# Loading each ranked expert's number into a SyncE register next to the first weight load that uses it

## The chip, the cores and the metric

The kernel runs on one core of one Trainium2 chip. The metric is the device time of one execution in microseconds (us); less is better. A number given for a kernel is the median of its runs. The profile is of one further execution, which has its own time.

## What is computed

The reference is a two-layer trunk over 256 latent tokens and 256 context tokens of width 1024, all in 32-bit floats. Layer 0 is attention and a dense SwiGLU; layer 1 is a short gated convolution and then a mixture of experts, which is the part that matters here:

```python
logits = h @ router_w                                  # 256 tokens x 8 experts
top_vals, top_idx = lax.top_k(logits, 2)
weights = softmax(top_vals)
gates = sum(one_hot(top_idx, 8) * weights[..., None])
for e in range(8):                                     # each expert: 1024 -> 3584 -> 1024
    out += gates[:, e] * ((silu(h @ w_gate[e]) * (h @ w_up[e])) @ w_down[e])
```

Each token uses two of the eight experts. All eight experts' weights, 352 MB of the 470 MB that the kernel reads, pass through the core once.

## The kernel before

**Experts by rank.** The experts are worked in the order of ranks 0 to 7. Rank 0 is always expert 0, so its weights can be read before the router's answer is there. Ranks 1 to 7 are the other experts, sorted by how many tokens chose them; ranks 0 to 4 are "heavy" (a tile of 128 tokens, weights split in two parts for exactness), ranks 5 to 7 "light" (64 tokens). Each expert is cut into 7 chunks. A list `chunks` fixes the order of the 56 chunks: four heavy chunks of rank 0, then heavy and light mixed, at last four light ones. So which rank comes when is known as the program is built; which expert a rank stands for is known only on the chip. The DVE computes it in `ranks` (L1165) into the tile `idx`, and SyncE (SP) needs it in registers to form the address of a weight load.

**Weight loads.** Every weight tile is a DMA of 1 MB, issued by SP with `load` (L61) into a buffer `raw` out of a ring of pools, in the fixed order of the list `order`: for each chunk two `moe_g` and two `moe_u` tiles, with two `moe_d` tiles of the chunk before. In `feed` (L110) an entry of `order` that is a function is called to give the source; `weights` (L91) makes these functions, which look the expert's register up in `who`. At one place the tiles named `xhat` and `late` and four buffers of further pools join the ring (L117), so that more loads can be in flight. A load waits for the last reader of its buffer's old content, and for the load eight places earlier to land. SP runs its instructions strictly in the order of the program.

**Conversion and matmuls.** A loaded tile of a heavy chunk is taken in two halves of 128x1024: ScalarE (ACT) writes a rounded part `hi` (L71), VectorE (DVE) the rest `lo` (L72), into five buffers, and TensorE (PE) multiplies `hi` and `lo` in groups of three matmuls at L267, L269 and L271. `ahead(4)` (L133) converts up to four halves before the one in use. Light chunks go straight to PE (L1316).

**The first chunk.** Chunk 0 has eight parts p = 0 to 7 on PE, one for each half tile: two for the first `moe_g` tile, two for the first `moe_u`, two for the second `moe_g`, two for the second `moe_u`. The first three of these tiles are loaded before the router's work is done. The hook at (0, 1) (L1412) runs `ranks` in part 1; with it, in the program's order, stand the seven loads of `idx` into registers. The hook at (0, 3) turns positions into rank order (`by_rank`, L1193), the one at (1, 1) computes the gates (`gates`, L1199), both small DVE work. The schedule is written by hand: each engine's order is the order of the code.

Of the kernel before, what the change touches and what calls it, by code (L numbers as in the profile page):

```python
# [19 lines left out]
NE = 8  # L20
# [13 lines left out]
def trunk(ctx, tc, i, out, dbg=None):  # L34
    nc = tc.nc
# [11 lines left out]
    cur = {}  # L47
# [4 lines left out]
    def pm():  # L52
        return cur["pm"].tile([128, 512], F32, name="pm")
# [35 lines left out]
    who, whole = {}, []  # L89

    def weights(m, r, c, h):  # L91
        return lambda: i[m][who[r] if r else 0, c, h]

    whole += [False] * len(order)
    for n in range(len(chunks) + 1):
        if n < len(chunks):
            order += [weights(m, *chunks[n], h) for h in range(2) for m in ("moe_g", "moe_u")]
            whole += [chunks[n][0] >= NE - NL] * 4
        if n:
            order += [weights("moe_d", *chunks[n - 1], h) for h in range(2)]  # L100
            whole += [chunks[n - 1][0] >= NE - NL] * 2
# [1063 lines left out]
    def ranks():  # L1165

        n = pm()
        pe.matmul(n[:, 0:8], ones, sl[:, 0], start=True, stop=False)
        pe.matmul(n[:, 0:8], ones, sl[:, 1], start=False, stop=True)
        key, rank, ids, long = (m1.tile([128, NE], F32, name=v) for v in ("key", "rnk", "ids", "long"))  # L1170
        cmp = m1.tile([128, NE, NE], F32, name="cmp")
        idx = m1.tile([128, NE], I32, name="idx")
        most = m1.tile([128, 1], F32, name="most")
        io = iota[:, 0:NE]
        dve.scalar_tensor_tensor(key, n[:, 0:8], 16.0, io, op0=OP.mult, op1=OP.subtract)
        dve.memset(key[:, 0:1], 1e6)
        dve.tensor_tensor(cmp, key[:, None, :].to_broadcast([128, NE, NE]), key[:, :, None].to_broadcast([128, NE, NE]),
                          op=OP.is_ge)
        dve.reduce_sum(rank, cmp, axis=AX.X)
        dve.tensor_tensor(perm, rank[:, None, :].to_broadcast([128, NE, NE]), io[:, :, None].to_broadcast([128, NE, NE]),  # L1180
                          op=OP.is_equal)
        dve.tensor_mul(cmp, perm, io[:, None, :].to_broadcast([128, NE, NE]))
        dve.reduce_sum(ids, cmp, axis=AX.X)
        dve.tensor_scalar(idx, ids, 1.0, None, op0=OP.subtract)
        for r in range(1, NE):
            who[r] = nc.values_load(idx[0:1, r:r + 1], engines=[mybir.EngineType.SP], min_val=0, max_val=NE - 1)
        dve.tensor_scalar(cap, rank, NE - NL + 0.5, CAP - 128.0, op0=OP.is_gt, op1=OP.mult)
        dve.tensor_scalar(cap, cap, 128.0, None, op0=OP.add)
        dve.tensor_tensor(long, n[:, 0:8], cap, op=OP.is_gt)
        dve.reduce_max(most, long, axis=AX.X)  # L1190
        dve.tensor_scalar(over, most, 0.5, None, op0=OP.is_gt)
# [205 lines left out]
    def down(C, s):  # L1397
# [10 lines left out]
        else:  # L1408
            k = slice(s * 128, (s + 1) * 128)
            mac(E.accs, C.dh[:, k], C.dl[:, k], *halves(ahead(4)), first, end)  # L1410

    hook(0, 1, ranks)  # L1412
    hook(0, 3, by_rank, posr, pos)
    hook(1, 1, gates)
# [4 lines left out]
    for n, (r, c) in enumerate(chunks):  # L1419
# [8 lines left out]
        for p in range(8):  # L1428
# [11 lines left out]
            half, m, j = p // 4, (p // 2) % 2, p % 2  # L1440
# [27 lines left out]
    for t in range(NT):  # L1468
        for q in range(2):
            c = slice(512 * q, 512 * q + 512)  # L1470
# [158 lines left out]
```

## Time and profile before

| what | us |
|---|---|
| median of 3 runs (1416.14, 1416.44, 1419.62) | 1416.44 |
| the profiled execution, its own time | 1419.48 |
| the profiled execution, span on the core | 1417.7 |
| PE busy (97% of the span) | 1380.8 |
| DVE busy (70%) | 990.7 |
| ACT busy (56%) | 791.0 |
| SP's one wait for the expert numbers, line 1186 | 51.4 |

The page gives the busy time of each engine over the span and, in 40 slices of 35.4 us, how busy each engine and the DMA were and how many GB/s they moved. PE is nearly always busy, and the chain of work that ended last is PE for 92% of the span. Where PE is idle is seen only in a narrower window; where a wait of SP shows, the question is whether PE needed what SP was about to load.

### The profile page before, as it was taken

What the parts mean: (1) busy time and instruction counts of PE and PEld (TensorE: products, weight loads), DVE (VectorE), ACT (ScalarE), POOL (GpSimd) and SP (SyncE); (2) the same over time, 40 slices, a digit from 0 to 9 for tenths busy, and PEclk for the clock granted to TensorE, in tenths of its full rate; (3) what the DMA queues carried; (4) which work ended last, traced back from release to release, by engine and by line L of the source; (5) the groups of instructions that cost most, each with busy time, mean ns of one, the idle gap of its engine ahead of it and who ended that gap; (6) DMA issues with size and microseconds to landing.
All of it is one profiled execution on the core that took longest, in us unless ns stands there. A gap on an engine that the chain in (4) does not pass through costs nothing.

```text
span 1417.7 us, 20577 instructions
## 1 busy us (share of the span) xinstructions
PE 1380.8 (97%) x7764; PEld 1020.5 (72%) x7764; DVE 990.7 (70%) x1341; ACT 791.0 (56%) x1070; POOL 0.2 (0%) x4
## 2 busy tenths in 40 slices
PE   6999999999999979999999999999999999999997
PEld 4776789999899968866666766767667676676742
DVE  4777769788777659866767767767577677676731
ACT  5567674444464348756556656656567566465610
POOL 0000000000000000000000000000000000000000
PEclk9999999999999989999999999999999999999999
DMA  9734778678756049999899999989989999998994
GB/s 368 275 120 132 255 297 298 237 300 306 254 222 254 31 166 421 421 421 421 367 423 421 420 406 368 401 340 386 420 335 413 420 415 371 359 420 368 411 421 171
DMA packets 66060, 469.81 MB, mean 331 GB/s; under 512 B 7328, under 2 KB 7968, under 8 KB 10016
## 3 DMA queue, kind: packets, MB, share of 16 engines
q1 hardware_dynamic: 65952, 468.41, 82.7%
q8 instruction: 63, 1.03, 0.3%
q14 instruction: 45, 0.37, 0.1%
HBM read 467.33 MB, written 1.05 MB: 330 GB/s over the span
## 4 chain that ended last, share of the span: by engine, by line
PE 92%; ACT 3%; DVE 3%; DMA 1%; issue 1%; SPq 0%; DVEq 0%; ACTq 0%
PE pm L1316 11%; PE pm L267 9%; PE pm L269 9%; PE pm L271 9%; PE acc L267 8%; PE acc L269 8%; PE acc L271 8%; PE acc L1316 5%; PE pm L923 4%; PE pm L925 4%; PE pm L924 4%; PE pm L1296 2%; PE pm L1258 2%; PE pm L177 1%; PE pm L1336 1%; PE pt L687 1%
## 5 line engine op out<-in xcount | busy, mean ns | idle before, releaser
L72 DVE TENSOR_TENSOR lo<-raw,hi 128x1024 fp32r<-128x1024 f32 x522 | 627.2, 1222 | 133.3 <-ACT hi L71 109.5
L71 ACT ACTIVATE hi<-raw 128x1024 fp32r<-128x1024 f32 x522 | 545.6, 1060 | 257.6 <-PE pm L271 113.0
L267 PE MATMUL pm<-hi,eh 128*128 128x512 f32 x560 | 225.6, 403 | 6.9 <-ACT hi L71 6.7
L269 PE MATMUL pm<-lo,eh 128*128 128x512 f32 x560 | 219.6, 392 | 2.1 <-DVE lo L72 2.1
L271 PE MATMUL pm<-hi,el 128*128 128x512 f32 x560 | 219.1, 391 | 0.0
L1316 PE MATMUL pm<-raw,hl 128*64 128x512 f32 x672 | 155.6, 599 | 0.0
L923 PE MATMUL pm<-th,hi 128*128 128x256 f32 x480 | 135.1, 281 | 0.0
L924 PE MATMUL pm<-tl,hi 128*128 128x256 f32 x480 | 134.6, 280 | 0.0
L925 PE MATMUL pm<-th,lo 128*128 128x256 f32 x480 | 134.6, 280 | 0.0
L267 PEld LDWEIGHTS pm<-hi,eh 128*128 128x128 f32 x560 | 105.5, 188 | 40.0 <-issue 8.8
L269 PEld LDWEIGHTS pm<-lo,eh 128*128 128x128 f32 x560 | 105.7, 189 | 24.7 <-DVE lo L72 4.6
L271 PEld LDWEIGHTS pm<-hi,el 128*128 128x128 f32 x560 | 105.5, 188 | 22.7
L1316 PEld LDWEIGHTS pm<-raw,hl 128*64 128x64 f32 x672 | 44.1, 136 | 79.8 <-issue 76.9
L923 PEld LDWEIGHTS pm<-th,hi 128*128 128x128 f32 x480 | 90.8, 189 | 1.2 <-issue 0.8
L924 PEld LDWEIGHTS pm<-tl,hi 128*128 128x128 f32 x480 | 90.7, 189 | 0.4
L925 PEld LDWEIGHTS pm<-th,lo 128*128 128x128 f32 x480 | 90.8, 189 | 0.0
L267 PE MATMUL acc<-hi,dh 128*128 128x512 f32 x280 | 88.6, 398 | 0.0
L269 PE MATMUL acc<-lo,dh 128*128 128x512 f32 x280 | 86.5, 390 | 0.0
L271 PE MATMUL acc<-hi,dl 128*128 128x512 f32 x280 | 86.3, 389 | 0.0
L1310 DVE TENSOR_TENSOR sg<-pm,sg 128x512 f32<-128x512 f32 (+1 forms) x56 | 38.6, 688 | 63.2 <-ACT sg L1309 62.9
L1316 PE MATMUL acc<-raw,dT 128*64 128x512 f32 x336 | 78.1, 600 | 0.0
L1309 ACT ACTIVATE sg<-pm 128x512 f32<-128x512 f32 (+1 forms) x56 | 32.8, 585 | 69.5 <-PE pm L1316 66.4
(323 smaller groups left out, 1646.4 us busy)
## 6 DMA issues: line engine op xcount, KB each, us to landing
raw<-in_moe_d_dram SPq DMA_DIRECT2D x112, 1024.0 KB, 11.2
raw<-in_moe_g_dram SPq DMA_DIRECT2D x111, 1024.0 KB, 11.5
raw<-in_moe_u_dram SPq DMA_DIRECT2D x111, 1024.0 KB, 11.0
raw<-in_ada_w_dram SPq DMA_DIRECT2D x48, 1024.0 KB, 6.3
raw<-in_conv_i_dram SPq DMA_DIRECT2D x12, 1024.0 KB, 6.9
raw<-in_ffn_g_dram SPq DMA_DIRECT2D x11, 1024.0 KB, 6.3
raw<-in_ffn_u_dram SPq DMA_DIRECT2D x11, 1024.0 KB, 5.1
raw<-in_ffn_d_dram SPq DMA_DIRECT2D x11, 1024.0 KB, 4.9
```

Of the source, the lines that this page charges most:

```text
L71: act.activation(hi, r, AF.Copy)
L72: dve.tensor_sub(lo, r, hi.bitcast(F32))
L267: pe.matmul(p, hh, wh[j], start=first, stop=False)
L269: pe.matmul(p, hh, wl[j], start=False, stop=False)
L271: pe.matmul(p, hl, wh[j], start=False, stop=last)
L923: pe.matmul(d, hi[:, c], th[:, k], start=(k == 0), stop=False)
L924: pe.matmul(d, hi[:, c], tl[:, k], start=False, stop=False)
L925: pe.matmul(d, lo[:, c], th[:, k], start=False, stop=(k == KD - 1))
L1258: pe.matmul(E.ps[:, k * 128:(k + 1) * 128], x[:, t, kk * 128:(kk + 1) * 128], E.os[:, t], start=(t == 0), stop=(t == NT - 1))
L1309: act.activation(sg, C.g, AF.Silu)
L1310: dve.tensor_mul(sg, C.u, sg)
L1316: pe.matmul(ps[m * CAP:(m + 1) * CAP], lhsT, w, start=first, stop=last, tile_position=(0, m * CAP))
```

## The change

`ranks` no longer loads the seven numbers itself; it leaves the tile `idx` in `cur["who"]`. The function that `weights` makes loads the number of a rank when it is called for that rank the first time, that is right ahead of the first weight load of that rank in SP's program.

```diff
     def weights(m, r, c, h):
-        return lambda: i[m][who[r] if r else 0, c, h]
+        def ap():
+            if r and r not in who:
+                who[r] = nc.values_load(cur["who"][0:1, r:r + 1], engines=[mybir.EngineType.SP], min_val=0, max_val=NE - 1)
+            return i[m][who[r] if r else 0, c, h]
+        return ap
@@
         dve.tensor_scalar(idx, ids, 1.0, None, op0=OP.subtract)
-        for r in range(1, NE):
-            who[r] = nc.values_load(idx[0:1, r:r + 1], engines=[mybir.EngineType.SP], min_val=0, max_val=NE - 1)
+        cur["who"] = idx
```

SP's program in the first chunk, before (a `TENSOR_LOAD` reads one number of `idx` into a register, the two `ISA` after it check it; a row's last part names the semaphores waited for, those of the DMAs, DVE or PE):

```order
L64 DMA raw<-in_moe_g_dram 128x2048 [waits DMAHW0_49,DVE_49]
L1186 TENSOR_LOAD idx [waits DVE_49]
L1186 ISA x2
L1186 TENSOR_LOAD idx
...
L64 DMA raw<-in_moe_u_dram 128x2048 [waits DMAHW2_49,DMAHW1_49,DVE_49]
L64 DMA raw<-in_moe_g_dram 128x2048 [waits DVE_49]
L117 DMA xhat<-in_moe_u_dram 128x2048 [waits DMAHW3_49]
L117 DMA raw<-in_moe_g_dram 128x2048 [waits DMAHW4_49,PE_49]
L117 DMA late<-in_moe_g_dram 128x2048 [waits DMAHW0_49]
L64 DMA raw<-in_moe_u_dram 128x2048 [waits DMAHW1_49,PE_49]
```

The same place in SP's program now:

```order
L64 DMA raw<-in_moe_g_dram 128x2048 [waits DMAHW0_49,DVE_49]
L64 DMA raw<-in_moe_u_dram 128x2048 [waits DMAHW2_49,DMAHW1_49,DVE_49]
L64 DMA raw<-in_moe_g_dram 128x2048 [waits DVE_49]
L121 DMA xhat<-in_moe_u_dram 128x2048 [waits DMAHW3_49]
L121 DMA raw<-in_moe_g_dram 128x2048 [waits DMAHW4_49,PE_49]
L121 DMA late<-in_moe_g_dram 128x2048 [waits DMAHW0_49]
L64 DMA raw<-in_moe_u_dram 128x2048 [waits DMAHW1_49,PE_49]
```

All seven `TENSOR_LOAD` are gone from here; each of the loads keeps its own waits. The first `TENSOR_LOAD` now stands 25 weight loads further on, and the other six after it, one at a time. At the second of them, in the mixed chunks, SP's program was, before:

```order
L64 DMA raw<-in_moe_d_dram 128x2048 [waits DMAHW0_49,DVE_49]
L64 DMA raw<-in_moe_d_dram 128x2048 [waits DMAHW1_49,PE_49]
L64 ISA
L64 DMA raw<-in_moe_g_dram 128x2048 [waits DMAHW2_49,DVE_49]
L64 DMA raw<-in_moe_u_dram 128x2048 [waits DMAHW3_49,PE_49]
L64 DMA raw<-in_moe_g_dram 128x2048 [waits DMAHW4_49,DVE_49]
```

and is now:

```order
L64 DMA raw<-in_moe_d_dram 128x2048 [waits DMAHW0_49,DVE_49]
L64 DMA raw<-in_moe_d_dram 128x2048 [waits DMAHW1_49,DVE_49]
L94 TENSOR_LOAD idx
L94 ISA x2
L64 ISA
L64 DMA raw<-in_moe_g_dram 128x2048 [waits DMAHW2_49,DVE_49]
L64 DMA raw<-in_moe_u_dram 128x2048 [waits DMAHW3_49,PE_49]
L64 DMA raw<-in_moe_g_dram 128x2048 [waits DMAHW4_49,PE_49]
```

Besides the `TENSOR_LOAD`, these four loads take the same four buffers in another order, which the waits show; after them the buffers are the same as before. The order of the instructions on PE, DVE and ACT, and what each waits for, is unchanged throughout.

## Rows read from the trace of the kernel before

**Rows 1.** Page, 40 slices of the span: GB/s that the DMA moved.

```profile
GB/s 368 275 120 132 255 297 298 237 300 306 254 222 254 31 166 421 421 421 421 367 423 421 420 406 368 401 340 386 420 335 413 420 415 371 359 420 368 411 421 171
```

**Rows 2.** Stretches: length, busy us (instructions) of PE, PEld, DVE, ACT, POOL; PEclk, DMA share, GB/s.

```profile
480.00:500.00 20.00, 19.42 (x133) 15.84 (x132) 12.38 (x31) 9.37 (x23) 0.00 (x0) 0.97 0.01 2
...
515.00:520.00 5.00, 0.47 (x3) 0.05 (x1) 0.00 (x0) 0.00 (x0) 0.00 (x0) 0.94 0.53 180
520.00:525.00 5.00, 2.35 (x5) 1.56 (x6) 2.73 (x6) 3.31 (x4) 0.00 (x0) 0.50 1.01 424
...
540.00:560.00 20.00, 20.00 (x94) 16.60 (x94) 19.60 (x19) 17.22 (x20) 0.00 (x0) 1.00 1.01 420
```

**Rows 3.** Waits of SP's queue, whole run: total us, times, longest.

```profile
SPq L1186 <- DVE long L1189: 51.4, 1, 51.4
```

**Rows 4.** SP in order of time: start, us, what it issued.

```profile
460.78 0.33 SPq L64 DMA_DIRECT2D raw<-in_moe_g_dram  x1
516.33 0.33 SPq L64 DMA_DIRECT2D raw<-in_moe_u_dram  x1
```

**Rows 5.** Instructions on tile idx: duration ns min/median/max, first and last start.

```profile
L1186 SPq TENSOR_LOAD <-idx x7: 262/263/469, 512.0 to 515.7; - x7
L1184 DVE TENSOR_SCALAR idx<-ids x1: 172/172/172, 511.8 to 511.8; 128x8 int32<-128x8 f32 x1
```

**Rows 6.** Waits from 500 to 560 us: total us, times, longest.

```profile
ACT hi L71 <- DMA raw<-in_moe_u_dram: 11.1, 1, 11.1
...
PE pm L267 <- ACT hi L71: 6.7, 1, 6.7
```

**Rows 7.** PE in order of time: start, us; in brackets idle time before, and its ender.

```profile
514.86 0.39 PE L269 MATMUL pm<-lo,eh 128*128 128x512 f32 x1
515.09 0.39 PE L271 MATMUL pm<-hi,el 128*128 128x512 f32 x1
522.19 0.80 PE L267 MATMUL pm<-hi,eh 128*128 128x512 f32 x1 [6.71 <-ACT hi L71]
523.45 0.80 PE L269 MATMUL pm<-lo,eh 128*128 128x512 f32 x1 [0.46 <-DVE lo L72]
...
526.17 0.43 PE L269 MATMUL pm<-lo,eh 128*128 128x512 f32 x1
...
536.03 0.50 PE L269 MATMUL pm<-lo,eh 128*128 128x512 f32 x1
```

**Rows 8.** DVE in order of time.

```profile
512.79 1.22 DVE L72 TENSOR_TENSOR lo<-raw,hi 128x1024 fp32r<-128x1024 f32 x1
522.17 1.23 DVE L72 TENSOR_TENSOR lo<-raw,hi 128x1024 fp32r<-128x1024 f32 x1 [8.16 <-ACT hi L71]
...
530.15 0.69 DVE L1310 TENSOR_TENSOR sg<-pm,sg 128x512 f32<-128x512 f32 x1 [0.18 <-ACT sg L1309]
531.10 1.23 DVE L72 TENSOR_TENSOR lo<-raw,hi 128x1024 fp32r<-128x1024 f32 x1 [0.26 <-ACT hi L71]
...
532.90 0.17 DVE L1206 TENSOR_TENSOR gts<-gts,sl 128x16 f32<-128x16 f32 x1 [0.28 <-ACT gts L1205]
...
534.76 3.48 DVE L72 TENSOR_TENSOR lo<-raw,hi 128x1024 fp32r<-128x1024 f32 x3
```

**Rows 9.** DVE and PE in order of time: last readers of buffers that the held loads fill.

```profile
462.19 3.61 DVE L233 SCALAR_TENSOR_TENSOR adav<-raw,spad,adav 128x256 f32<-128x256 f32 x7
...
479.16 0.28 PE L925 MATMUL pm<-th,lo 128*128 128x256 f32 x1
...
497.86 1.07 PE L177 MATMUL acc<-raw,spad 128*32 128x256 f32 x16
```

**Rows 10.** PE by line from 545 to 1400 us: busy us, mean ns, idle before, its ender.

```profile
L269 PE MATMUL pm<-lo,eh 128*128 128x512 f32 x528 | 206.2, 391 | 1.6 <-DVE lo L72 1.6
```

**Rows 11.** Instructions on tile over: duration ns min/median/max, first and last start.

```profile
L1477 SPq TENSOR_LOAD <-over x1: 277/277/277, 1384.3 to 1384.3; - x1
```

**Rows 12.** Page, DMA issues: number, KB each, median us from issue to landing.

```profile
raw<-in_moe_d_dram SPq DMA_DIRECT2D x112, 1024.0 KB, 11.2
```

## The prediction

> **What bounds the kernel now.** I read the slices of the page first, because the chain and the busy shares only say "PE". The DMA moves 31 and 166 GB/s in slices 14 and 15 (460.8 to 531.6 us) and about 420 GB/s right after [rows 1]: the loads stop while the router works. The waits of SP's queue say why: one wait of 51.4 us, at the line that reads the expert numbers into registers [rows 3]. The row names a DVE instruction of line 1189 as its ender; the order in time is clearer: `idx` is written at 511.8, the first register load starts at 512.0 and the last at 515.7 [rows 5]. In between SP issues nothing: one weight load at 460.78, the next at 516.33 [rows 4].
>
> Next, whether PE needed those loads. It did, a little: ACT waited 11.1 us for the load issued at 516.33 (the second `moe_u` tile of chunk 0), and PE 6.7 us for ACT [rows 6]. PE's last matmul before the gap starts at 515.09, the next at 522.19; after that gap PE is slow for 4 us [rows 7], at a granted clock of 0.50, its lower level of 1.2 GHz, from 520 to 525 [rows 2]. From 545 to 1400 us the largest idle time on PE is 1.6 us, before the `lo` matmuls [rows 10]. So PE is the bound, with one hole at 515 to 527, and what moves PE forward there should move the end by as much.
>
> **The change part by part.**
>
> *The seven register loads leave the first chunk.* From the first at 512.0 to the next weight load at 516.33 they take 4.3 us of SP, 0.6 us each with their two checks [rows 4, 5]. More than that, the wait for `idx` ahead of them goes, and behind it stood the loads. What holds these loads then? Each keeps its own waits, for the last reader of its buffer, so I take those from the trace. The first needs a buffer that the DVE finishes at 462.19 + 3.61 = 465.8; four need the matmuls of the convolution, done at 479.16 + 0.28 = 479.4; the last readers on PE of the conditioning weights end at 497.86 + 1.07 = 498.9 [rows 9]. The first load had landed and been rounded by ACT when the DVE took it at 522.17, so within 5.8 us of its issue [rows 4, 8]. Issued at about 466 it is there by 472, over 35 us before it is wanted; the whole batch that was issued between 516 and 521 has landed by about 500. The DMA is idle in that time (0.01 share from 480 to 500 [rows 2]), so nothing is pushed aside.
>
> *What PE gains.* Two engines can be last once the loads are there.
>
> PE itself: its gap from the end of the slot of the matmul at 515.09 (matmuls start 0.23 apart at full clock, 514.86 to 515.09) to 522.19 is 6.87 us. From 522.19 to 526.17 it starts seven matmuls, which take 7 x 0.23 = 1.6 at full clock and took 3.98, so 2.4 are lost to the low clock and to a wait of 0.46 for `lo` [rows 7]. Another 0.2 is lost ahead of 536.03. If PE alone decided, it would gain 6.9 + 2.4 + 0.2 = 9.5 us.
>
> The DVE: it makes the `lo` halves, and from 522.17 on it works nearly without a break; 19.6 of 20 us are busy from 540 to 560 [rows 2]. Three conversions in a row take 3.48, so they start (3.48 - 1.22) / 2 = 1.13 apart. With its tile there, the conversion at 522.17 follows the one at 512.79 directly, at 513.92: 8.25 us earlier [rows 8]. All DVE work behind it moves by that. Of its three short waits after this (0.18, 0.26 and 0.28 [rows 8]) the first two are for ACT, which ran late because of the same loads; they may go, 0.44 in all. The third is an exchange with ACT inside the gates and stays. The first `lo` of the group at 534.76 is what PE waits for at 536.03 [rows 7, 8].
>
> So at 536.03 PE comes 8.25 to 8.7 us earlier by the DVE and 9.5 by itself; the later of the two decides: 8.25 to 8.7. I take **8.4**. PE will wait about 1 us for the DVE in these 15 us; this is the stall that takes the old one's place, and it is inside the 8.4. After 540 PE runs dense, so the shift stays.
>
> *Does the DMA keep up?* It is saturated from 540 on (1.01 share [rows 2]), and PE would come 8.4 us earlier. But the DMA has then carried some ten loads already, 25 us of work at 420 GB/s, in time that was idle, so every later load is issued when its buffer is free, 8.4 us earlier than now, and lands no later than that. No cost.
>
> *The seven register loads in their new places.* Each costs SP 0.6 us ahead of a weight load [rows 4, 5]. SP mostly waits for buffers there, and a load lands 11.2 us (median) after its issue, of which 1.05 MB at 420 GB/s are 2.5 us of its own: 8.7 us of other loads are in the queue ahead of it [rows 2, 12]. A delay of 0.6 is hidden under these. If that cover were gone, it would be 7 x 0.6 = 4.2 us at most. The trace shows no register load with the DMA saturated; the nearest is SP's at 1384.3, with the last weights in flight: 0.277 us, against 0.262 to 0.469 for those with the DMA idle [rows 5, 11]. I take zero.
>
> The Trainium skill, "DMA: Bandwidth & Descriptors", section "Latency and other measured facts", gives a `tensor_load` a floor of about 600 ns and says that the compiler unrolls them by four to spread that cost. By this rule seven in one place are better than seven singly, against the change. The row disagrees on the figure (0.26 us for most), and the sum would be the same 4.2 us at most.
>
> *The four buffers in another order.* The second register load's neighbours take the same four buffers, and each load has the same 8.7 us of queue ahead of it. Nothing.
>
> *The sum.* 1419.48 - 8.4 = 1411.1 for an execution like the profiled one (span 1417.7 - 8.4 = 1409.3). The median of before is 3.0 lower than that execution; taken from it, 1416.44 - 8.4 = **1408.0 us**.
>
> **The rivals.**
>
> *PE alone decides:* the DVE finds more slack than I see and PE gains its 9.5, 1406.9. For it: ACT and DVE were both late because of one load. Against it: DVE works back to back.
>
> *Given back:* PE, 8.4 us earlier, meets loads that cannot come earlier because the DMA has been saturated for long stretches. For it: 420 GB/s in many slices [rows 1]. Against it: the head start of 50 us, and slices at 340 to 400 between the full ones, in which the DMA waited for buffers. How much would be lost no row tells, from none to all 8.4; the middle is 4.2, 1412.2.
>
> *Single register loads cost:* the 4.2 us come on the path, 1416.44 - 8.4 + 4.2 = 1412.2. For it: each stands ahead of a load that SP could issue at once. Against it: SP's queue is ahead of the landings. The skill's rule named above speaks for this one; its 600 ns would give 4.2 as well.
>
> *It does not do what it says:* the loads are held by something else and start no earlier, so 1416.4. Their waits end at 465.8 to 498.9 [rows 9], which leaves little room for this.
>
> *Slower:* a register load on SP waits behind the weight loads in flight when the DMA is saturated, as a load does, 11.2 us. SP then issues nothing for 11.2 + 0.3, the queue of 8.7 runs dry, and the DMA stands 2.8 us, seven times 19.6 us; less the 8.4 that is 1427.6. It decides from 8.7 + 8.4 / 7 = 9.9 us for one register load, twenty times the longest seen. Against it is the 0.277 at 1384.3 [rows 11].
>
> **How the numbers follow.** Forecast 0.72, PE alone 0.08, given back 0.07, single loads cost 0.05, does not do what it says 0.05, slower 0.03. The runs of before lie up to 3.2 us above their median, so a median of after can too. The range takes in 9.5 of gain and a little of that scatter below, 1405.5, and the two cases at 1412.2 above, 1412.4. A measurement of this kernel tells about 0.3%, 4.2 us, from no change: faster than 1412.2 are the forecast, PE alone and half of the two cases that end on the bound, 0.86; within, the other half and the case without effect, 0.11; slower 0.03.
>
> **What would show it.** In the profile of after: SP's wait at the register line of 51.4 us is gone, and weight loads start at about 466, 467, 467.5 and then at 479 and 493; slice 14 moves 200 GB/s or more and not 31. ACT's wait of 11.1 us for the DMA and PE's 6.7 us are gone; the granted clock from 515 to 530 is 1.00. The DVE has no pause of 8 us at 514. PE has short waits for `lo` between 516 and 528, about 1 us together. The register loads last under 0.6 us wherever they stand. What PE did at 536.03 it does at about 527.6, and the last matmul, the end of ACT and DVE all move by the same 8.4. I am wrong if the shift at 540 is there and is smaller at 1400 (given back), if weight loads are still missing at 480, or if a register load lasts several us.

## The result, and the profile after

| | before | after |
|---|---|---|
| median of 7 runs each, us | 1416.44 | 1407.87 |
| lowest and highest, us | 1413.77, 1420.81 | 1404.37, 1411.53 |
| ratio of the times, 95% interval | | 0.9939 (0.9919 to 0.9959) |
| span of the profiled execution, us | 1417.7 | 1406.1 |

The change makes the kernel 8.6 us faster; 1408.0 was forecast.

SP comes first. Its order of time (start, us, what it issued) answers to [rows 4]; where one load stood at 460.78 and the next at 516.33, there are now these, with other lines left out:

```profile
457.71 0.33 SPq L64 DMA_DIRECT2D raw<-in_moe_g_dram  x1
462.76 0.33 SPq L64 DMA_DIRECT2D raw<-in_moe_u_dram  x1
464.10 0.33 SPq L64 DMA_DIRECT2D raw<-in_moe_g_dram  x1
464.48 0.42 SPq L121 DMA_DIRECT2D xhat<-in_moe_u_dram  x1
476.28 0.33 SPq L121 DMA_DIRECT2D raw<-in_moe_g_dram  x1
...
490.09 0.33 SPq L64 DMA_DIRECT2D raw<-in_moe_u_dram  x1
```

The load that ACT had waited for is issued at 462.76 and no longer at 516.33, and no wait of ACT for the DMA is left between 505 and 560 us. Between the loads at 476.28 and 490.09 stand four more; of these the orders shown for this place under "The change" have only the last, `late`. The page's GB/s line (40 slices of 35.2 us) and the instructions on tile `idx` answer to [rows 1] and [rows 5]:

```profile
GB/s 372 277 120 141 250 298 301 240 299 301 251 235 261 275 281 351 286 422 382 343 422 421 420 390 383 378 362 376 421 345 421 413 414 363 364 420 370 411 420 167
```

```profile
L94 SPq TENSOR_LOAD <-idx x7: 268/276/488, 544.6 to 1176.5; - x7
```

Slices 14 and 15 move 275 and 281 GB/s where 31 and 166 stood. The seven register loads lie between 544.6 and 1176.5 us and take 0.27 to 0.49 us each.

Next PE, in order of time, against [rows 7], and the stretches of 515 to 525 and of 530 to 545 (columns as in [rows 2]). Line 273 is line 269 of before:

```profile
513.86 0.39 PE L271 MATMUL pm<-hi,eh 128*128 128x512 f32 x1
514.36 0.50 PE L273 MATMUL pm<-lo,eh 128*128 128x512 f32 x1
514.70 0.40 PE L275 MATMUL pm<-hi,el 128*128 128x512 f32 x1
...
523.88 0.39 PE L271 MATMUL pm<-hi,eh 128*128 128x512 f32 x1
524.28 0.50 PE L273 MATMUL pm<-lo,eh 128*128 128x512 f32 x1
```

```profile
515.00:520.00 5.00, 5.00 (x27) 4.21 (x26) 5.00 (x6) 4.22 (x5) 0.00 (x0) 1.00 0.98 356
520.00:525.00 5.00, 4.98 (x24) 3.83 (x23) 4.44 (x15) 4.10 (x6) 0.00 (x0) 1.00 0.19 79
...
530.00:545.00 15.00, 15.00 (x73) 12.45 (x72) 14.86 (x15) 12.77 (x16) 0.00 (x0) 1.00 0.94 351
```

The hole is gone: PE no longer waits 6.7 us, and the granted clock stays at 1.00. Matmuls start 0.23 apart, so the one at 514.36, 0.50 behind its forerunner, is 0.27 late, and the one at 524.28, 0.40 behind, 0.17 late. Both wait for `lo`, from the DVE. The matmul at 524.28 is the one that stood at 536.03 [rows 7].

**A common mark.** On PE, ACT and DVE the two kernels run the same program up to the moment at which the DVE writes `idx`, but that moment is not the same in two executions: in the profiles shown here and below it lies between 505.4 and 513.1 us. In the profile of after it came at 508.96, in that of before at 511.84, and 2.88 us of the difference of the two spans are of this kind. They are older than the change: the last weight load ahead of those that it moves already stands 3.07 us apart (460.78 and 457.71). One thing that differs from execution to execution is the granted clock. These are the same 32 matmuls ahead of `idx`, behind the same wait, in the profile of before and in that of behind1, a kernel of the experiments below:

```profile
500.63 6.25 PE L1258 MATMUL pm<-os,x 128*128 128x128 f32 x32 [0.74 <-DVE os L1231]
```

```profile
496.97 3.81 PE L1267 MATMUL pm<-os,x 128*128 128x128 f32 x32 [0.74 <-DVE os L1240]
```

The granted clock from 500 to 505 us is 0.50 in the first and 1.00 in the second. Four of the twelve profiles took 3.81 us here and the other eight 5.5 to 6.5. So I count from `idx` written to the start of the last group of matmuls, in every kernel. Three lines do it, in order of time; the first is of before, the second and third of after:

```profile
1408.07 1.99 PE L1467 MATMUL pm<-raw,ohTl 64*128 64x512 f32 x8 [0.85 <-DVE raw L1463]
```

```profile
508.96 0.17 DVE L1188 TENSOR_SCALAR idx<-ids 128x8 int32<-128x8 f32 x1
1396.26 1.99 PE L1470 MATMUL pm<-raw,ohTl 64*128 64x512 f32 x8 [0.85 <-DVE raw L1466]
```

Before, 1408.07 - 511.84 = 896.23 us; after, 1396.26 - 508.96 = **887.30**: the change gains 8.93 us. At the matmul of 536.03 and 524.28 it is 24.19 - 15.32 = 8.87. So the whole gain is made within 25 us of `idx`, and the 872 us that follow take as long as before, to 0.06 us.

### The profile page after: what moved, and what is told of

Read it like the earlier page. It is cut to its first block, busy times and chain, and to the rows that moved or that the text cites. A ratio compares the mean times of both kernels' runs of the same rounds, so it can differ in the third digit from the quotient of the medians.

```text
span 1406.1 us, 20577 instructions
## 1 busy us (share of the span) xinstructions
PE 1375.2 (98%) x7764; PEld 1017.2 (72%) x7764; DVE 990.2 (70%) x1341; ACT 791.2 (56%) x1070; POOL 0.2 (0%) x4
## 3 DMA queue, kind: packets, MB, share of 16 engines
HBM read 467.33 MB, written 1.05 MB: 333 GB/s over the span
## 4 chain that ended last, share of the span: by engine, by line
PE 93%; ACT 3%; DVE 3%; issue 1%; DMA 0%; DVEq 0%; ACTq 0%
PE pm L1319 11%; PE pm L271 9%; PE pm L273 9%; PE pm L275 9%; PE acc L271 8%; PE acc L273 8%; PE acc L275 8%; PE acc L1319 5%; PE pm L927 4%; PE pm L929 4%; PE pm L928 4%; PE pm L1299 2%; PE pm L1261 2%; PE pm L181 1%; PE pm L1339 1%; PE pt L691 1%
```

## The experiments

Each kernel below differs from the changed kernel by the lines shown. "From the mark" is the time from `idx` written to the start of the last group of matmuls in its profile, 896.23 before and 887.30 with the change. Before had medians of 1417.20, 1418.21 and 1417.24 us on the three occasions, beside which the ratios stand.

| kernel | `idx` written, us | last group, us | from the mark, us | median, us | ratio to before (95%) |
|---|---|---|---|---|---|
| bunch | 509.19 | 1396.49 | 887.30 | 1408.18 | 0.9932 (0.9908 to 0.9956) |
| every | 508.95 | 1397.30 | 888.35 | 1409.77 | 0.9940 (0.9919 to 0.9962) |
| one_early | 509.75 | 1403.36 | 893.61 | 1415.25 | 0.9985 (0.9965 to 1.0005) |
| behind1 | 505.73 | 1401.49 | 895.76 | 1416.19 | 0.9994 (0.9980 to 1.0008) |
| behind2 | 511.09 | 1402.43 | 891.34 | 1412.59 | 0.9953 (0.9938 to 0.9967) |
| behind3 | 511.63 | 1399.19 | 887.56 | 1412.38 | 0.9955 (0.9938 to 0.9972) |
| behind1_fill | 505.36 | 1399.12 | 893.76 | 1415.69 | 0.9983 (0.9966 to 0.9999) |
| late_small | 506.54 | 1396.54 | 890.00 | 1410.09 | 0.9948 (0.9932 to 0.9965) |
| gates_p6 | 513.13 | 1400.11 | 886.98 | 1409.07 | 0.9939 (0.9921 to 0.9957) |
| both_later | 508.20 | 1394.92 | 886.72 | 1406.67 | 0.9930 (0.9905 to 0.9954) |

Each time from the mark is that of one profile. What lies behind the first chunk repeats closely: from the first matmul `acc<-hi,dh` (540.04 before, 528.27 after) to the last group nine of the twelve profiles take 867.98 to 868.03 us. What lies ahead of it repeats to 0.01 us in the change, bunch and every; how far a stretch at the lower clock in it repeats is not known, as each such kernel has one profile. The medians' intervals are 4 to 7 us wide and can bear out the large differences only.

The theory: what counts is that the wait for `idx` no longer stands ahead of the first few weight loads. The rivals: it is the time of the register loads themselves that left the first chunk; single loads in their new places cost something that the gain hides; a gain beyond what the DVE allows is still to be had.

### bunch: all seven together, at the first use

```diff
-            if r and r not in who:
-                who[r] = nc.values_load(cur["who"][0:1, r:r + 1], ...)
+            if r and not who:
+                for q in range(1, NE):
+                    who[q] = nc.values_load(cur["who"][0:1, q:q + 1], ...)
```

> All seven register loads stand together right ahead of the first weight load that needs one of them, 25 weight loads behind their old place. Measure: time from the writing of idx to the start of the last matmuls (896.2 us before, 887.3 after). Held loads (the gain is the weight loads that stood behind SP's wait for idx): 887.3 +- 0.5, as with single register loads, time 1408. Register time (the gain is the 4.3 us of the seven register loads): 887.3 too, if SP has room there. Single loads cost: up to 4 us better than the change, 883 to 887.

From the mark 887.30, the same as the change to 0.01 us. Seven in one place (from 544.9 to 548.5) or one by one makes no difference; it is their place ahead of the held loads that they must leave.

### every: 294 register loads

```diff
-            if r and r not in who:
+            if r:
```

> The number is read again ahead of every weight load of ranks 1 to 7, 294 register loads in place of 7, each 0.6 us on SP. Held loads: SP waits for buffers there and its loads land long after issue, so nothing: 887.3 +- 0.5, time 1408. Single loads cost: 287 more at 0.6 us are 172 us on SP; if a tenth of that came on the path, 17 us, time 1425.

The instructions on tile `idx` in this kernel:

```profile
L94 SPq TENSOR_LOAD <-idx x294: 262/268/482, 544.6 to 1369.6; - x147
```

One ahead of every weight load of ranks 1 to 7: 287 more than with the change, 0.6 us of SP each with its checks, as in [rows 4, 5], some 172 us of SP in all. From the mark the kernel takes 1.05 us more, less than 4 ns for each. This falls in one place, where PE does not wait with the change:

```profile
844.36 0.47 PE L271 MATMUL pm<-hi,eh 128*128 128x512 f32 x1 [1.14 <-DVE xhat L1346]
```

Whether the register loads cause this wait is not shown; everywhere else SP's time is covered wholly, and seven cost nothing that can be seen.

### one_early: one of the seven stays

```diff
         cur["who"] = idx
+        who[5] = nc.values_load(idx[0:1, 5:6], ...)
```

> One register load stays at the old place, the other six go to their first uses: the wait for idx stays, six sevenths of the register time go. Held loads: the first held load is issued at 0.8 us after idx in place of 4.5, so 3.7 us earlier, plus some of the 2.4 us lost to the low clock: idx to last matmuls 890.1 to 892.5, time 1410.5 to 1412.7. Register time: six sevenths of the whole gain, 888.6, time 1409.

One register load in the old place gives back 6.31 of 8.93 us, though it takes 0.47 us: the first held load goes out at 510.84, 1.09 us after `idx`. That is the theory, but 893.61 is 1.1 us beyond what I expected. PE in order of time, and the stretch of 515 to 525:

```profile
516.71 0.79 PE L271 MATMUL pm<-hi,eh 128*128 128x512 f32 x1 [3.32 <-ACT hi L71]
517.97 0.80 PE L273 MATMUL pm<-lo,eh 128*128 128x512 f32 x1 [0.46 <-DVE lo L72]
518.56 0.63 PE L275 MATMUL pm<-hi,el 128*128 128x512 f32 x1
518.99 0.63 PE L271 MATMUL pm<-hi,eh 128*128 128x512 f32 x1
...
523.26 0.44 PE L273 MATMUL pm<-lo,eh 128*128 128x512 f32 x1
523.54 0.40 PE L275 MATMUL pm<-hi,el 128*128 128x512 f32 x1
```

```profile
515.00:520.00 5.00, 2.83 (x6) 1.93 (x7) 3.21 (x7) 3.87 (x4) 0.00 (x0) 0.65 1.01 426
520.00:525.00 5.00, 5.00 (x20) 4.01 (x18) 4.89 (x5) 4.46 (x6) 0.00 (x0) 0.66 1.02 431
```

The pause is half as long as before (3.32 us against 6.71 [rows 6, 7]), but matmuls start 0.43 apart and not 0.23 for 6.5 us after it, against 4.0 us in [rows 7]. I had let the slow stretch shrink with the pause. 3.32 + 0.46 + (6.55 - 0.46) x (1 - 0.23/0.43) = 6.6 us, less the 0.45 that PE waits for `lo` with the change anyway, is 6.2 of the 6.31.

### behind1, behind2, behind3: how many loads must get past

The seven register loads and their wait go back into the first chunk, behind one, two or three of the loads that the change sets free (N is 1, 2 or 3).

```diff
+                if cur.get("left"):
+                    cur["left"] -= 1
+                    if not cur["left"]:
+                        for q in range(1, NE):
+                            who[q] = nc.values_load(cur["who"][0:1, q:q + 1], ...)
                 if whole[u]:
@@
         cur["who"] = idx
+        cur["left"] = N
```

> The seven register loads, with the wait for idx, stand in the first chunk behind one of the weight loads that they held, ahead of the second. Held loads: the second load lands where the first one did, PE gets two halves (12 matmuls, 2.7 us) further and then stops; idx to last matmuls 893.0 to 893.5 (896.2 before, 887.3 after), time 1413. Register time: the 4.3 us are still there, 896.2.

> The same behind two of the held loads. Held loads: the third lands about 2.9 us later than it is wanted, idx to last matmuls about 890.2, time 1410.5. Register time: 896.2.

> The same behind three of the held loads. Held loads: the fourth lands just when it is wanted, so the whole gain is there with the wait and the seven register loads still in the first chunk: 887.3 to 887.8, time 1408. Register time: 896.2.

With three loads past, the time from the mark is 887.56, within 0.26 us of the change, and yet all seven register loads take their 4 us of SP in the first chunk. Instructions on `idx` and SP's order of time in behind3:

```profile
L128 SPq TENSOR_LOAD <-idx x7: 263/265/467, 511.8 to 515.5; - x7
```

```profile
465.62 0.33 SPq L64 DMA_DIRECT2D raw<-in_moe_u_dram  x1
466.97 0.33 SPq L64 DMA_DIRECT2D raw<-in_moe_g_dram  x1
467.35 0.42 SPq L121 DMA_DIRECT2D xhat<-in_moe_u_dram  x1
516.10 0.33 SPq L121 DMA_DIRECT2D raw<-in_moe_g_dram  x1
```

SP stands still from 467 to 516 here, much as before, and it costs 0.26 us. That settles two points: the time of the register loads is no cause, and neither are the 50 us in which the DMA rests; what counted were three tiles that came too late. The medians say less: that of behind3 is 5.8 us below before's, and its ratio agrees with the change's only within the intervals (0.9955 against 0.9939).

One load past (behind1) is not enough, and is worse than I expected by over 2 us. ACT waits 8.9 us for the next tile. PE in order of time, the DVE, and the stretches of 515 to 530:

```profile
512.15 0.40 PE L280 MATMUL pm<-hi,el 128*128 128x512 f32 x1
516.21 0.80 PE L276 MATMUL pm<-hi,eh 128*128 128x512 f32 x1 [3.66 <-ACT hi L71]
...
525.32 0.60 PE L276 MATMUL pm<-hi,eh 128*128 128x512 f32 x1
525.75 0.41 PE L278 MATMUL pm<-lo,eh 128*128 128x512 f32 x1
```

```profile
516.19 2.36 DVE L72 TENSOR_TENSOR lo<-raw,hi 128x1024 fp32r<-128x1024 f32 x2 [5.12 <-ACT hi L71]
```

```profile
515.00:520.00 5.00, 3.33 (x8) 2.34 (x9) 3.65 (x4) 4.36 (x5) 0.00 (x0) 0.55 1.01 426
520.00:525.00 5.00, 5.00 (x16) 4.23 (x17) 3.84 (x9) 4.69 (x6) 0.00 (x0) 0.50 1.00 421
525.00:530.00 5.00, 5.00 (x24) 4.09 (x23) 4.86 (x11) 4.09 (x6) 0.00 (x0) 0.92 1.02 426
```

The DVE's wait for ACT is 5.1 us here, 3.1 shorter than the 8.16 of [rows 8], so the DVE alone would have let 3.1 us be gained. But PE works at a granted clock of 0.50, the lower level of 1.2 GHz, for 9.1 us after a pause of 3.66 us, and so PE is the later of the two: 3.66 + 0.46 + (9.11 - 0.46) x (1 - 0.23/0.43) = 8.1 us, less 0.45 that the change waits too, is 7.7 of the 8.46 that behind1 takes longer than the change. The rest is open.

Two loads past (behind2) lie between, 891.34, a little over 1 us beyond my figure: PE waits 0.76 us for `lo` and 0.90 for the DVE's `sg`, and after that its matmuls start 0.43 apart for 3.7 us.

### behind1_fill: is it the clock?

behind1, with 16 matmuls whose result nothing reads, put where PE pauses. They add work and change no output.

```diff
         for p in range(8):
+            if n == 1 and p == 0:
+                fill = acc()
+                for _ in range(16):
+                    pe.matmul(fill, E.eh[0][:, 0], E.eh[0].rearrange("p k c -> p (k c)"), start=True, stop=True)
             run(n, p)
```

> behind1 again (seven register loads behind one of the held weight loads; idx to last matmuls 895.8 us, where 893.0 to 893.5 was expected), with 16 matmuls of 128x512 into an unused PSUM tile in PE's pause of 3.7 us; they add 3.6 us of work that nobody reads. Low clock (behind1 lost its gain to TensorE's lower clock after the pause): the granted clock stays 1.00 after the pause, and the DVE's three conversions and small steps that are already done (3.2 us) show as gain: 892.8 to 893.6. No effect of the clock (the DVE or the DMA holds PE there anyway): 895.8 or more.

PE in order of time, and the stretches of 515 to 525:

```profile
512.01 3.81 PE L1441 MATMUL acc<-eh 128*128 128x512 f32 x16
515.90 0.49 PE L276 MATMUL pm<-hi,eh 128*128 128x512 f32 x1
517.16 0.50 PE L278 MATMUL pm<-lo,eh 128*128 128x512 f32 x1 [0.77 <-DVE lo L72]
...
527.16 0.50 PE L278 MATMUL pm<-lo,eh 128*128 128x512 f32 x1 [1.49 <-DVE lo L72]
```

```profile
515.00:520.00 5.00, 4.16 (x21) 3.05 (x20) 3.94 (x4) 4.45 (x5) 0.00 (x0) 1.00 1.02 428
520.00:525.00 5.00, 5.00 (x25) 4.06 (x24) 3.80 (x10) 4.69 (x7) 0.00 (x0) 1.00 1.01 428
```

The 16 matmuls fill the pause, the first matmul behind it comes as early as in behind1 (10.54 us after `idx` against 10.48), the clock stays at 1.00, and 2.0 us are gained from the mark by adding 3.8 us of unread work. PE then waits 0.77 and 1.49 us for `lo`: without the low clock the DVE is last, as the working by the DVE says. 893.76 is just outside what I expected. So in these two executions the low clock behind the pause is the cause of 2.0 of the 2.3 to 2.8 us by which behind1 missed. They are alike up to the pause (the 32 matmuls ahead of `idx` take 3.81 us in both). The medians do not tell the two kernels apart (0.9994 and 0.9983, with intervals that overlap), so how much a run gains as a rule stays open; the two fastest runs of each lie over 2 us apart as well (1413.01 and 1413.04 against 1410.73 and 1410.81).

### late_small, gates_p6, both_later: is there more to gain?

With the change PE still waits 0.45 us for the DVE. In these three kernels the small DVE work (`by_rank`, `gates`) moves out of the way:

```diff
     hook(0, 1, ranks)
-    hook(0, 3, by_rank, posr, pos)
-    hook(1, 1, gates)
+    hook(1, 5, by_rank, posr, pos)
+    hook(2, 1, gates)
```

for late_small; in gates_p6 `gates` is at (1, 6) and `by_rank` stays, in both_later they stand at (1, 4) and (1, 7).

> The changed kernel, with the small DVE work of by_rank in chunk 1 in place of 0 and of gates in chunk 2 in place of 1. If the DVE is what holds PE in the 15 us after the old gap, PE's two waits for lo there (about 0.4 us together) go: idx to last matmuls 886.8 to 887.1. If the waits only move with the work: 887.3. If the DVE is too full in the later place (it is busy nearly all the time from 530 to 550): 887.5 to 889.

> The changed kernel, with gates in part 6 of chunk 1 in place of part 1, by_rank left where it is. The DVE holds PE at the end of the 15 us after the old gap: PE's second wait for lo (about 0.2 us, 15 us after idx) goes, and nothing comes later, as there are a dozen us to the first use of the gates: idx to last matmuls 887.0 to 887.2 (887.3 for the change). If the work only moves a wait: 887.3 to 888.

> The same with by_rank in part 4 and gates in part 7 of chunk 1. If PE's two waits for lo (0.3 and 0.2 us) both go: 886.8 to 887.0. If the DVE is then late for the gates or for the weights' conversions: 887.3 to 889.

late_small was a miss. PE's waits for `lo` go, and a new one comes, for what `gates` makes, in order of time:

```profile
534.89 0.90 PE L1287 MATMUL pm<-gtsr,oh 128*128 128x1 f32 x4 [1.29 <-DVE gtsr L1200]
...
537.06 0.63 PE L275 MATMUL pm<-hi,el 128*128 128x512 f32 x1
537.49 1.05 PE L1299 MATMUL pm<-cid,sg 128*128 128x128 f32 x4
```

`gates` comes too late for PE's line 1287: PE waits 1.29 us, and some 1.8 us after the wait its matmuls start 0.43 apart until 540.05. In all it is 2.7 us worse than the change. A little earlier is right: 886.98 with `gates` at (1, 6) and 886.72 with both moved. In both_later nothing is left of PE's waits, from 505 to 545:

```profile
505.00:545.00 40.00, 40.00 (x187) 32.78 (x186) 38.79 (x63) 34.33 (x39) 0.00 (x0) 1.00 0.80 301
```

PE is busy for 40.00 of 40 us. This is the best of the kernels, 0.58 us below the change from the mark; its median of 1406.67 does not tell it apart from the change.

## Why the prediction was right

**The loads' own waits.** Right. The loads were to start at about 466, 467, 467.5, 479 and 493. Less the 2.88 us that this execution was ahead, that is 463.1, 464.1, 464.6, 476.1 and 490.1; they start at 462.76, 464.10, 464.48, 476.28 and 490.09.

**The DVE decides.** Right. The conversion that stood at 522.17, 10.33 us after `idx` [rows 5, 8], is the second of the pair that begins at 509.92 in these rows of the DVE, in order of time:

```profile
509.92 2.35 DVE L72 TENSOR_TENSOR lo<-raw,hi 128x1024 fp32r<-128x1024 f32 x2
...
516.49 2.35 DVE L72 TENSOR_TENSOR lo<-xhat,hi 128x1024 fp32r<-128x1024 f32 x2
518.76 0.68 DVE L1313 TENSOR_TENSOR sg<-pm,sg 128x512 f32<-128x512 f32 x1
519.36 1.22 DVE L72 TENSOR_TENSOR lo<-raw,hi 128x1024 fp32r<-128x1024 f32 x1
...
521.14 0.17 DVE L1209 TENSOR_TENSOR gts<-gts,sl 128x16 f32<-128x16 f32 x1 [0.28 <-ACT gts L1208]
...
523.02 3.48 DVE L72 TENSOR_TENSOR lo<-raw,hi 128x1024 fp32r<-128x1024 f32 x3
```

It starts at 509.92 + 2.35 - 1.22 = 511.05, 2.09 after `idx`: 8.24 us earlier, where 8.25 was worked out.

**The DVE's short waits: the term that was mis-sized.** From that conversion to the group that PE waits for (534.76 before, 523.02 after) the DVE took 12.59 us and now takes 11.97. The step gave 0 to 0.44 for this and took 0.15; it measured 0.62. Both waits for ACT went, as the step allowed, and the exchange inside the gates stayed (0.28 then and now). But a wait costs more than its bracket says. In the rows above `sg` starts at 518.76 while the conversions ahead of it run to 516.49 + 2.35 = 518.84, and the next conversion starts at 519.36, before `sg` ends at 519.44: instructions of the DVE in a row overlap by 0.08 us, and a wait between them loses that too. 0.18 + 0.08 + 0.26 + 0.08 = 0.60, which is nearly the 0.62. So the gain is 8.24 + 0.62 = 8.86 at the matmul of 524.28, just above the 8.25 to 8.7 of the sum.

**PE alone.** 9.5 was its bound, and PE falls 9.5 - 8.87 = 0.6 us short of it and not 1: its new waits for the DVE are 0.27 + 0.17, about 0.45, and the matmul behind the first of them starts 0.34 and not 0.23 later. This is the same term, seen from PE.

**The DMA keeps up.** Right; "given back" is refuted by the 872 us behind the mark, which take as long as before to 0.06 us. There is slack now: the DMA's share from 530 to 545, with PE dense, is 0.94, where [rows 2] have 1.01 from 540 to 560; from 520 to 525 it is 0.19.

**Register loads in new places.** Zero was right: the 872 us in which they now stand take as long as before, bunch shows no difference, and the 287 more of every show at one place at most. That also refutes the rival of 4.2 us and, with the longest at 0.488 us, the slower one. The Trainium skill, "DMA: Bandwidth & Descriptors", section "Latency and other measured facts", gives a `tensor_load` about 600 ns at the least; 262 to 492 ns are measured here, with the DMA idle and with it saturated (262 to 272 in every from 700 to 820 us, at a share of 1.01), so the trace differs. What the same section says of the compiler, that it unrolls them by four to spread that cost, finds nothing to spread here, as bunch and every show.

**The time.** 8.93 us from the mark against 8.4; the medians differ by 8.57. The forecast of 1408.0 agrees with 1407.87 better than its parts do: 0.5 us of the mis-sized term is below what the medians can tell.

## What to carry to other kernels

A wait on a queue that issues its work strictly in order, as SP's 51.4 us here, holds everything behind it, also work that has nothing to do with the wait; a load of a value into a register belongs right ahead of its first use, or at least behind the transfers that the next stage needs first (three of them were enough here). The gain of such a step is what the second engine in line allows, so work it out for each engine that was late and take the least. When two executions differ by some us in stages that the change does not touch, compare them from a common mark inside the program, and look at the granted clock ahead of it.

## What was not expected of the hardware

A shorter pause of PE can be followed by more time at the lower clock. All within 25 us of `idx`, with the time for which matmuls then started 0.43 apart and not 0.23 (in the first three a wait of 0.46 for `lo` lies in that time):

| kernel | PE's pause, us | then at the lower clock, us |
|---|---|---|
| before | 6.71 | 4.0 |
| behind1 | 3.66 | 9.1 |
| one_early | 3.32 | 6.5 |
| behind2 | 0.76, then 0.90 | 3.7 |
| behind1_fill | filled; later 0.77 and 1.49 | none |

In late_small a wait of 1.29 us, 28 us after `idx`, was followed by 3.4 us. What sets the length these runs do not show, and each row is one execution: ahead of `idx`, around the same wait of 0.74 us, the clock fell in eight of the twelve profiles and not in the other four, so another execution of these kernels may have other lengths. They show that a gain by a shorter pause of PE can't be read off the pause alone, and that unread matmuls in the pause kept the clock at 1.00 and gained 2.0 us in the one pair of profiles.
